# Memory values made token-major after a scan, and local attention with keys and values split once and scaled on VectorE

## The chip, the cores and the metric

The kernel runs on one core of one Trainium2 chip. The metric is device time in microseconds for one execution of the whole program; three runs were timed, and one further execution was profiled. The engines are called as the profile calls them: PE (TensorE matmul), PEld (its weight load), DVE (VectorE), ACT (ScalarE), POOL (GpSimd), SP (SyncE, which issues all the transfers spoken of here).

## What is computed

One encoder layer in float32 on 1024 tokens of width 1024, with 256 memory tokens. The parts that the change touches:

```python
# (A) local attention: 8 heads of 64 in 2 groups of 4, one key and value head per group,
#     blocks of 128 tokens, each block sees itself and its two neighbours, +-128 tokens
scores = einsum('bnqhgd,bnkhd->bnhgqk', qb, kw) * (64 ** -0.5)
m = maximum(max(scores), sink); p = exp(scores - m)
denom = sum(p) + exp(sink - m)
o = einsum('bnhgqk,bnkhd->bnqhd', p / denom, vw)
# (B) gated delta rule, both directions, a scan over chunks
mix = concatenate([attn_o, dn_o]) @ w_out;  x = x + rms_norm(mix)
# cross-attention into the memory tokens
kv = rms_norm(mem) @ w_ckv          # 1024 -> 2048: keys, then values
k, v = kv[..., :1024], kv[..., 1024:]
p = softmax(einsum('bqhd,bkhd->bhqk', q, k) / 16);  c = einsum('bhqk,bkhd->bqhd', p, v) @ w_co
# then a dense SwiGLU
```

## The kernel before, in words

**Precision.** Every large product is made of three products of rounded parts. `split` (L99) writes a rounded copy `hi` on ACT (L102) and the rest `lo = src - hi` on DVE, or on POOL where the caller says so (L103). A product is hi·hi + hi·lo + lo·hi.

**Weights.** `load_w` (L118) loads a block of 512 KB into `wraw` (L125), splits it to `whi` and `wlo`. All three have two buffers, which all matrices share: a third load waits until the first block's split is done, a third split until PE has used the first. `load_w` runs at a raised priority (L120), so its instructions are placed ahead of what stands before them in the program.

**Order.** The program is written as steps in lists (`ORDER_1`, L36, to `ORDER_3`, L38); a scheduler then orders each engine's instructions, and each engine works its list strictly in order and waits at the first instruction whose input or buffer is not ready. In `ORDER_2`, `V` makes the values and `A0` to `A4` the rotated queries and keys of local attention and store them to `d_v`, `d_q`, `d_k`; `W` starts two windows. In `ORDER_3`, `M` normalises and turns the memory tokens into `mT` (two parts, depth on the partitions), `s01` advances both scans by a step, `W` is again two windows, `K` makes one block of the memory's keys or values.

**Local attention** (`window`, L598) works on one block of 128 queries and one group: 16 windows, group 0 first. A window loads its two or three blocks of keys (`kr`, twice, for both halves of the partitions, L610), of queries (`qr`, twice, L611) and of values (`vr`, L613), splits them (`khi` L616, `klo` L617, `vhi` L621, `vlo` L622, `qs` L624 and L625), makes the scores of four heads (`psw`, L633), reduces them on DVE with the mask (L635), takes the exponentials on ACT (L642), the sum (`es`, L645 to L648), and scales the probabilities on ACT (L650). After the `yield` they are turned on PE (`ptw`, L656), split (`ph`, `pl`) and multiplied by the values (`pow`, L661), and the result is stored to `d_mix` (`ao`, L664 to L666). `next_windows` (L668) starts a window before it finishes the one before. The values are kept twice side by side (`vhi` has a dimension of 2), so that `pow` has 128 rows.

**Scan** (`scan`, L749): eight steps for two pairs of heads. Each loads `kv` and `pz`, multiplies 128x128 blocks (`psc`, L763) and updates the state on DVE.

**Keys and values of the memory** (`next_kv`, L883): block `ct` takes 128 columns of `w_ckv` (L125, rows of 512 bytes). The weights are the stationary operand and `mT` with its 256 tokens moves (`pck`, L891): 24 matmuls of 256 columns give a block with 128 features on the partitions. ACT copies it (`cv`, L893). Keys (blocks 0 to 7) go to `d_mk` like that. Values (blocks 8 to 15) are needed with tokens on the partitions, so PE turns them (`ptv`, L899), ACT copies again (`vv`, L901) and SP stores them (L902). `ORDER_3` has eight `K` between the scan steps and eight behind them.

**What follows.** `mid_gemm` (L967) multiplies the mixer's output by `w_out` (`pmg`, L984). Its operand is `d_mix`, loaded (`mraw`, L1023) and split to `b0` to `b3`. Then `mkr` and `mvr` are loaded from `d_mk` and `d_mv` (L1035) and split to `kr` and `vr`, the operands of cross-attention; `gpost` (L961) and `xr` (L994) are loads of a gain and of `x`.

Of the kernel before, what the change touches and what calls it, by code (L numbers as in the profile page):

```python
# [19 lines left out]
P = 128  # L20
S = 1024
D = 1024
KT = D // P
NT = S // P
HALF = 512
# [4 lines left out]
ML = 256  # L30
# [4 lines left out]

ORDER_1 = "D0 P0 D1 P1 D2 P2 D3 P3 B0 B1".split()  # L36
ORDER_2 = "G0 G1 G2 G3 L0 L1 V A4 A0 A1 W L2 L3 W W A2 A3 W".split()
ORDER_3 = ("M " + "s01 W K " * 5 + "s01 K " * 2 + "s01 K s01 " + "K " * 8).split()  # L38


_NAMES = ["ident", "mUi", "mLi", "m5", "m6", "band0", "band1", "band2", "mU", "mL", "ones"]
# [34 lines left out]
def tile_hybrid_block(  # L76
# [31 lines left out]
    def pool(name, bufs, **kw):  # L108
        return tc.tile_pool(name=name, bufs=bufs, reuse_waits="tile", **kw)
# [20 lines left out]


    ident = cst.tile([P, P], F32, name="ident")
# [389 lines left out]
    def levels(h):  # L522
# [72 lines left out]

        together([part(b) for b in range(2)])

    def window(n, g):  # L598

        tok = slice(n * P, (n + 1) * P)  # L600
        k0, k1 = max(n - 1, 0), min(n + 1, NT - 1) + 1
        nb = k1 - k0
        w = nb * P
        band = C[:, _AT["band0"] - C0 + (k0 - n + 1) * P:][:, 0:w]


        kr = tw.tile([P, 384], F32, tag="kr", name="kr", bufs=1)[:, 0:w]
        qr = tw.tile([P, 4, P], F32, tag="qr", name="qr", bufs=1)
        for r in range(2):
            nc.sync.dma_start(kr[64 * r:64 * r + 64], d_k[64 * g:64 * g + 64, k0 * P:k1 * P])  # L610
            nc.sync.dma_start(qr[64 * r:64 * r + 64], d_q[256 * g:256 * g + 256, tok].rearrange("(h e) t -> e h t", h=4))  # L611
        vr = tw.tile([P, 3, 64], F32, tag="vr", name="vr", bufs=1)[:, 0:nb]
        nc.sync.dma_start(vr, d_v[k0:k1, :, 64 * g:64 * g + 64].rearrange("c p e -> p c e"))  # L613
        khi = tw.tile([P, 384], F32R, tag="khi", name="khi")[:, 0:w]
        klo = tw.tile([P, 384], F32R, tag="klo", name="klo", bufs=1)[:, 0:w]
        nc.scalar.copy(khi, kr)  # L616
        nc.gpsimd.tensor_tensor(klo, kr, f32(khi), ALU.subtract)  # L617
        vhi = tw.tile([P, 3, 2, 64], F32R, tag="vhi", name="vhi")[:, 0:nb]
        vlo = tw.tile([P, 3, 2, 64], F32R, tag="vlo", name="vlo")[:, 0:nb]
        v2 = bc(vr, 2, (P, nb, 2, 64))  # L620
        nc.scalar.copy(vhi, v2)  # L621
        nc.gpsimd.tensor_tensor(vlo, v2, f32(vhi), ALU.subtract)  # L622
        qs = tw.tile([P, 4, P], F32R, tag="qs", name="qs")
        nc.scalar.copy(qs, qr)  # L624
        nc.gpsimd.tensor_tensor(qs[64:128], qr[64:128], f32(qs[64:128]), ALU.subtract)  # L625

        m4 = tw.tile([P, 4], F32, tag="m4", name="m4")
        ssum = tw.tile([P, 4], F32, tag="ssum", name="ssum")
        pr = []
        for hh in range(4):  # L630
            pp = pw.tile([P, 512], F32, tag="pw", name="psw")
            for i, kk in enumerate((khi, klo)):
                nc.tensor.matmul(pp[:, 0:w], qs[:, hh, :], kk, start=(i == 0), stop=(i == 1))  # L633
            sc = tw.tile([P, 384], F32, tag="sc", name="sc", bufs=8)
            nc.vector.tensor_tensor_reduce(out=sc[:, 0:w], in0=pp[:, 0:w], in1=band, scale=0.125,  # L635
                                           scalar=sink[:, 4 * g + hh:4 * g + hh + 1], op0=ALU.add, op1=ALU.max,
                                           accum_out=m4[:, hh:hh + 1])
            pr.append(sc)
        nm = tw.tile([P, 4], F32, tag="nm", name="nm")
        nc.vector.tensor_scalar(nm, m4, -1.0, None, ALU.mult)  # L640
        for hh in range(4):
            nc.scalar.activation(pr[hh][:, 0:w], pr[hh][:, 0:w], AF.Exp, bias=nm[:, hh:hh + 1],  # L642
                                 accum_out=ssum[:, hh:hh + 1])
        es = tw.tile([P, 4], F32, tag="es", name="es")
        nc.gpsimd.tensor_tensor(es, sink[:, 4 * g:4 * g + 4], m4, ALU.subtract)  # L645
        nc.scalar.activation(es, es, AF.Exp)
        nc.vector.tensor_tensor(es, es, ssum, ALU.add)
        nc.vector.reciprocal(es, es)  # L648
        for hh in range(4):
            nc.scalar.mul(pr[hh][:, 0:w], pr[hh][:, 0:w], es[:, hh:hh + 1])  # L650
        yield
        po = pw.tile([P, 4, P], F32, tag="pow", name="pow", bufs=1)
        for j in range(nb):
            pp = pw.tile([P, 512], F32, tag="pw", name="ptw")
            for hh in range(4):
                nc.tensor.transpose(pp[:, hh * P:(hh + 1) * P], pr[hh][:, j * P:(j + 1) * P], ident)  # L656
            ph = tw.tile([P, 512], F32R, tag="ph", name="ph")
            pl = tw.tile([P, 512], F32R, tag="pl", name="pl")
            split(ph, pl, pp)
            for i, (vv, pe_) in enumerate(((vhi, ph), (vhi, pl), (vlo, ph))):  # L660
                nc.tensor.matmul(po.rearrange("p h t -> p (h t)"), vv[:, j].rearrange("p r e -> p (r e)"), pe_,  # L661
                                 start=(j == 0 and i == 0), stop=(j == nb - 1 and i == 2))
        ao = tw.tile([P, 2, P], F32, tag="ao", name="ao", bufs=1)
        nc.scalar.copy(ao[0:64], po[0:64, 0:4:2, :])  # L664
        nc.scalar.copy(ao[64:128], po[64:128, 1:4:2, :])
        nc.sync.dma_start(d_mix[g * 256:(g + 1) * 256, tok].rearrange("(k p) t -> p k t", p=P), ao)  # L666

    def next_windows():  # L668

        for _ in range(2):  # L670
            last = wins[-1] if wins else None
            if wins_done[0] < 2 * NT:
                wins.append(window(wins_done[0] % NT, wins_done[0] // NT))
                next(wins[-1])
            wins_done[0] += 1
            if last:
                next(last, None)

    wins, wins_done = [], [0]
    kqv = {0: kqv0}  # L680
# [15 lines left out]
    pw = p12.enter_context(pool("pw", 2, space=PSUM, side="right"))  # L696
    ps = pgs.enter_context(pool("psl", 2, space=PSUM))
    tw = p12.enter_context(pool("tw", 2))
    tl_ = p1.enter_context(pool("tl", 2))

    def attn_proj(ct):
# [179 lines left out]
    kv_done = [0]  # L881

    def next_kv():  # L883

        ct = kv_done[0]
        kv_done[0] += 1
        whi, wlo = load_w(w_ckv[:, ct * P:(ct + 1) * P], KT, P, nc.gpsimd if ct < KT else nc.vector)
# [5 lines left out]
        nc.scalar.copy(cv, pp)  # L893
        if ct < KT:
            nc.sync.dma_start(d_mk[ct * P:(ct + 1) * P, :], cv)
            return
        pt = pc.tile([P, 512], F32, tag="pc", name="ptv")[:, 0:ML]
        for t in range(2):
            nc.tensor.transpose(pt[:, t * P:(t + 1) * P], cv[:, t * P:(t + 1) * P], ident)  # L899
        vv = mk.tile([P, 2, P], F32, tag="vv", name="vv", bufs=2)  # L900
        nc.scalar.copy(vv, pt.rearrange("p (t n) -> p t n", t=2))  # L901
        nc.sync.dma_start(d_mv[:, :, (ct - KT) * P:(ct - KT + 1) * P].rearrange("t p n -> p t n"), vv)  # L902

    scans = [scan(g) for g in range(2)]

    def scan_step(pairs):

        for _ in range(4):
            for s_ in pairs:
                next(s_, None)  # L910

    issue(ORDER_3, {"s": lambda *gs: scan_step([scans[g] for g in gs]), "W": next_windows, "M": memory_norm,
                    "K": next_kv})
    dump("d_pz", d_pz[0] + d_pz[1])
    dump("d_kv", d_kv)
    dump("d_mix", d_mix)
# [454 lines left out]
```

## Time and profile before

| | us |
|---|---|
| median of the 3 runs | 1644.9 (1640.13 to 1646.33) |
| the profiled execution | 1638.65, of which 1636.9 is the span |
| PE busy over the span | 1556.8 (95%) |
| PEld, DVE, ACT, POOL busy | 1305.8, 948.6, 753.1, 547.6 |
| mean granted clock of TensorE | 0.984 |
| first scores of local attention (L633) | 354.1 |
| last value block of the memory (`ptv`, L899) | 619.4 |
| first matmuls of `w_out` (`pmg`, L984) | 619.5 |

The times of the profile are counted from the start of its span. A row of a group of instructions gives line, engine, operation, output and input, then busy time, mean duration of one in ns, idle time of the engine just before them and what ended it. In the timeline a row gives start, duration, engine, line, what it does, and in brackets the idle time before it. The granted clock is a share of full speed. "DMA share" is the mean busy share of the core's 16 transfer engines.

### The profile page before, as it was taken

The numbers are of one execution on the slowest core, as the hardware profiler recorded it, in microseconds if no ns is written. First come the engines' busy times: TensorE is split into PE (matmuls) and PEld (weight loads), VectorE is DVE, ScalarE is ACT, GpSimd is POOL, SyncE is SP. The second block draws the span as 40 slices with busy tenths as digits, with TensorE's granted clock in tenths as the row PEclk, the third lists the DMA queues.
The fourth block names the chain that finished last, engine by engine and source line by source line (L and its number), as shares of the span: only waits on it lengthen the run. The fifth ranks groups of instructions, "written<-read, shape, count | busy, mean of one in ns | idle before, by whom it ended". The sixth has DMA issues, their size and how long they took to land.

```text
span 1636.9 us, 21688 instructions
## 1 busy us (share of the span) xinstructions
PE 1556.8 (95%) x7802; PEld 1305.8 (80%) x7802; DVE 948.6 (58%) x1431; ACT 753.1 (46%) x1530; POOL 547.6 (33%) x501
## 2 busy tenths in 40 slices
PE   6999889998899979999999999999999999999998
PEld 5878778777799877788888777788888888888886
DVE  6855986966678844444346458776555553334332
ACT  6556552236758773554335565233333232444211
POOL 2467552334337500253202221343433441221100
PEclk9999999997999999999999999999999999999999
DMA  6134257574999583454213164442222223565452
GB/s 200 41 116 130 64 167 207 155 176 125 323 315 294 151 288 110 153 182 146 73 65 116 52 217 151 122 135 78 77 91 92 82 84 111 204 213 184 140 173 75
DMA packets 275560, 240.49 MB, mean 147 GB/s; under 512 B 43240, under 2 KB 226941, under 8 KB 275453
## 3 DMA queue, kind: packets, MB, share of 16 engines
q1 hardware_dynamic: 275453, 239.11, 47.0%
q8 instruction: 61, 1.00, 0.2%
q14 instruction: 46, 0.38, 0.1%
HBM read 177.69 MB, written 58.75 MB: 144 GB/s over the span
## 4 chain that ended last, share of the span: by engine, by line
PE 56%; DVE 2%; ACT 1%; issue 1%; DMA 1%; POOL 0%; SPq 0%; POOLq 0%; ACTq 0%; DVEq 0%
PE pmg L984 9%; PE pd L1325 7%; PE pd L1301 7%; PE pD L1155 7%; PE pE L1155 7%; PE pA L1155 6%; PE pcq L260 5%; PE pB L1155 3%; PE pcs L1064 1%; PE pco L1090 1%; DMA wraw<-in_w_gate_up_dram 1%; DVE wlo L103 0%; PE ptn L953 0%; PE pct L1080 0%; ACT xr L1001 0%
## 5 line engine op out<-in xcount | busy, mean ns | idle before, releaser
L102 ACT CAST whi<-wraw 128x1024 fp32r<-128x1024 f32 x108 | 113.1, 1049 | 163.8 <-issue 60.7
L103 POOL TENSOR_TENSOR wlo<-wraw,whi 128x1024 fp32r<-128x1024 f32 x48 | 118.3, 2465 | 173.3 <-ACT whi L102 157.0
L260 PE MATMUL pg<-hhi,whi 128*128 128x512 f32 x352 | 141.0, 402 | 0.0
L260 PE MATMUL pg<-hhi,wlo 128*128 128x512 f32 x352 | 140.3, 399 | 0.0
L260 PE MATMUL pg<-hlo,whi 128*128 128x512 f32 x352 | 140.0, 398 | 0.0
L103 DVE TENSOR_TENSOR wlo<-wraw,whi 128x1024 fp32r<-128x1024 f32 x60 | 74.5, 1244 | 87.5 <-ACT whi L102 83.4
L984 PE MATMUL pmg<-whi,b 128*128 128x512 f32 x384 | 117.7, 396 | 2.9 <-ACT whi L102 2.7
L1155 PE MATMUL pA<-b,whi 128*128 128x512 f32 x352 | 109.5, 392 | 1.3 <-ACT m L1172 1.3
L285 DVE SCALAR_TENSOR_TENSOR acc<-cp,cols,acc 128x1024 f32<-128x1024 f32 x48 | 75.8, 1580 | 34.2 <-ACT acc L283 33.6
L984 PEld LDWEIGHTS pmg<-whi,b 128*128 128x128 f32 x384 | 72.0, 190 | 18.6 <-ACT whi L102 3.5
L1232 POOL TENSOR_TENSOR act<-act,up 128x512 f32<-128x512 f32 x33 | 48.4, 1468 | 108.0 <-issue 58.4
L260 PEld LDWEIGHTS pg<-hhi,wlo 128*128 128x128 f32 x352 | 67.3, 191 | 13.4
L260 PEld LDWEIGHTS pg<-hhi,whi 128*128 128x128 f32 x352 | 67.3, 192 | 13.1 <-ACT hhi L102 0.3
L260 PEld LDWEIGHTS pg<-hlo,whi 128*128 128x128 f32 x352 | 67.1, 191 | 13.1
L1155 PEld LDWEIGHTS pA<-b,whi 128*128 128x128 f32 x352 | 65.3, 188 | 15.0 <-ACT m L1172 2.0
L984 PE MATMUL pmg<-wlo,b 128*128 128x512 f32 x192 | 71.6, 394 | 0.4 <-DVE wlo L103 0.4
L1155 PE MATMUL pA<-b,wlo 128*128 128x512 f32 x176 | 68.7, 391 | 1.0 <-DVE wlo L103 1.0
L1325 PE MATMUL pd<-wdh,ath 128*128 128x512 f32 x176 | 69.5, 395 | 0.0
L1325 PE MATMUL pd<-wdh,atl 128*128 128x512 f32 x176 | 69.4, 395 | 0.0
L1325 PE MATMUL pd<-wdl,ath 128*128 128x512 f32 x176 | 69.4, 395 | 0.0
L1301 PE MATMUL pd<-dl,whi 128*128 128x512 f32 x176 | 68.5, 389 | 0.0
L1301 PE MATMUL pd<-dh,wlo 128*128 128x512 f32 x176 | 68.3, 389 | 0.0
(390 smaller groups left out, 4189.6 us busy)
## 6 DMA issues: line engine op xcount, KB each, us to landing
wraw<-in_w_gate_up_dram SPq DMA_DIRECT2D x52, 512.0 KB, 4.2
kv<-d_kv SPq DMA_DIRECT2D x32, 512.0 KB, 6.5
wraw<-in_w_in_dram SPq DMA_DIRECT2D x22, 512.0 KB, 4.0
araw<-d_act SPq DMA_DIRECT2D x22, 512.0 KB, 3.3
draw<-in_w_down_dram SPq DMA_DIRECT2D x22, 512.0 KB, 4.1
atr<-d_act SPq DMA_DIRECT2D x16, 704.0 KB, 4.7
d_act<-act SPq DMA_DIRECT2D x40, 256.0 KB, 2.8
d_kv<-kv SPq DMA_DIRECT2D x8, 1024.0 KB, 6.4
```

Source lines behind the costliest of these rows:

```text
L102: nc.scalar.copy(hi, src)
L103: (eng or nc.vector).tensor_tensor(lo, src, f32(hi), ALU.subtract)
L260: nc.tensor.matmul(p_, w[:, k, :], ah[a][:, k, :], start=(k == 0 and i == 0), stop=(k == nk - 1 and i == 2))
L285: nc.vector.scalar_tensor_tensor(acc, cp[:, t:t + S], taps[t], acc, ALU.mult, ALU.add)
L984: nc.tensor.matmul(pp[t], act[a][:, k, tt], w_[:, kk, :], start=(k == 0 and i == 0), stop=(k == KT - 1 and i == 2))
L1064: nc.tensor.matmul(pp[:, t2_, :], q[a][:, ct, tt], kr_[b_][:, ct, :], start=(j == 0 and i == 0), stop=(j == 1 and i == 2))
L1090: nc.tensor.matmul(po, vr_[a][:, kt, cs], pts[kt][b_], start=(kt == 0 and i == 0), stop=(kt == 1 and i == 2))
L1155: nc.tensor.matmul(out_, w[a][:, k, :], xx[b_][:, k, :], start=(start and k == 0 and i == 0), stop=(k == HK - 1 and i == 2), skip_group_ch ...
L1232: nc.gpsimd.tensor_tensor(o_, o_, up, ALU.mult)
L1301: nc.tensor.matmul(pps[t], a[:, tt], b_, start=(f == 0 and i == 0), stop=(f == NF - 1 and i == 2))
L1325: nc.tensor.matmul(pp, a[:, f - f0], b_[:, f], start=(f == 0 and i == 0), stop=(f == NF - 1 and i == 2))
```

## The change

Three things, in one diff (cut; line numbers of the new file differ).

1. The values of the memory are made with tokens on the partitions: `mT` is the stationary operand, 512 columns of `w_ckv` move; two steps `V`, of four weight blocks of 256 rows by 512 columns each, stand behind the scan in place of eight `K`. There is no turn; `vv` has one buffer.
2. Keys and values of local attention are loaded and split in halves of 512 tokens for a group (`window_keys`), into tiles that stay; windows read slices. Keys, values and queries share the buffers `wr`, two of them. The values are no longer doubled, and `pow` has 64 rows.
3. The probabilities are scaled by `tensor_scalar` on DVE.

```diff
-ORDER_3 = ("M " + "s01 W K " * 5 + "s01 K " * 2 + "s01 K s01 " + "K " * 8).split()
+ORDER_3 = ("M " + "s01 W K " * 5 + "s01 K " * 3 + "s01 V V").split()
...
+    def window_keys(g, hf):
+        ts, cs = slice(hf * HALF, (hf + 1) * HALF), slice(4 * hf, 4 * hf + 4)
+        kr = tw.tile([P, HALF], F32, tag="wr", name="kr")
+        for r in range(2):
+            nc.sync.dma_start(kr[64 * r:64 * r + 64], d_k[64 * g:64 * g + 64, ts])
+        nc.scalar.copy(khi[:, ts], kr)
+        nc.gpsimd.tensor_tensor(klo[:, ts], kr, f32(khi[:, ts]), ALU.subtract)
+        vr = tw.tile([P, HALF], F32, tag="wr", name="vr")[:, 0:256].rearrange("p (c e) -> p c e", c=4)
+        nc.sync.dma_start(vr, d_v[cs, :, 64 * g:64 * g + 64].rearrange("c p e -> p c e"))
+        nc.scalar.copy(vhi[:, cs], vr)
+        nc.gpsimd.tensor_tensor(vlo[:, cs], vr, f32(vhi[:, cs]), ALU.subtract)
...
     def window(n, g):
...
-        kr = tw.tile([P, 384], F32, tag="kr", name="kr", bufs=1)[:, 0:w]
-        qr = tw.tile([P, 4, P], F32, tag="qr", name="qr", bufs=1)
+        qr = tw.tile([P, 4, P], F32, tag="wr", name="qr")
         for r in range(2):
-            nc.sync.dma_start(kr[64 * r:64 * r + 64], d_k[64 * g:64 * g + 64, k0 * P:k1 * P])
             nc.sync.dma_start(qr[64 * r:64 * r + 64], d_q[256 * g:256 * g + 256, tok].rearrange("(h e) t -> e h t", h=4))
-        vr = tw.tile([P, 3, 64], F32, tag="vr", name="vr", bufs=1)[:, 0:nb]
...
-                nc.tensor.matmul(pp[:, 0:w], qs[:, hh, :], kk, start=(i == 0), stop=(i == 1))
+                nc.tensor.matmul(pp[:, 0:w], qs[:, hh, :], kk[:, ks], start=(i == 0), stop=(i == 1))
...
-            nc.scalar.mul(pr[hh][:, 0:w], pr[hh][:, 0:w], es[:, hh:hh + 1])
+            nc.vector.tensor_scalar(pr[hh][:, 0:w], pr[hh][:, 0:w], es[:, hh:hh + 1], None, ALU.mult)
...
-                nc.tensor.matmul(po.rearrange("p h t -> p (h t)"), vv[:, j].rearrange("p r e -> p (r e)"), pe_,
+                nc.tensor.matmul(po.rearrange("p h t -> p (h t)"), vv[:, k0 + j], pe_,
...
     def next_windows():
         for _ in range(2):
             last = wins[-1] if wins else None
...
+                for hf in range(2) if n == 0 else ():
+                    window_keys(0, hf)
...
+            if n in (NT - 2, NT):
+                window_keys(1, n == NT)
...
+    khi, klo = (tw.tile([P, S], F32R, tag=t, name=t, bufs=1) for t in ("khi", "klo"))
+    vhi, vlo = (tw.tile([P, NT, 64], F32R, tag=t, name=t, bufs=1) for t in ("vhi", "vlo"))
...
-        pt = pc.tile([P, 512], F32, tag="pc", name="ptv")[:, 0:ML]
+    def next_values():
+        ch = kv_done[1]
+        kv_done[1] += 1
+        pp = [pc.tile([P, 512], F32, tag="pc", name="pcv") for _ in range(2)]
+        for kp in range(4):
+            whi, wlo = load_w(w_ckv[kp * 256:(kp + 1) * 256, D + ch * 512:D + (ch + 1) * 512], 2, 512)
+            for t in range(2):
+                for kk in range(2):
+                    k = 2 * kp + kk
+                    for i, (w, a) in enumerate(((whi, 0), (whi, 1), (wlo, 0))):
+                        nc.tensor.matmul(pp[t], mT[a][:, k, t * P:(t + 1) * P], w[:, kk, :], start=(k == 0 and i == 0),
+                                         stop=(k == KT - 1 and i == 2))
         for t in range(2):
-            nc.tensor.transpose(pt[:, t * P:(t + 1) * P], cv[:, t * P:(t + 1) * P], ident)
-        vv = mk.tile([P, 2, P], F32, tag="vv", name="vv", bufs=2)
-        nc.scalar.copy(vv, pt.rearrange("p (t n) -> p t n", t=2))
-        nc.sync.dma_start(d_mv[:, :, (ct - KT) * P:(ct - KT + 1) * P].rearrange("t p n -> p t n"), vv)
+            vv = mk.tile([P, 512], F32, tag="vv", name="vv", bufs=1)
+            nc.scalar.copy(vv, pp[t])
+            nc.sync.dma_start(d_mv[t, :, ch * 512:(ch + 1) * 512], vv)
```

More of the change, by code (lines that the diff above doesn't have):

```diff
@@ L604, in window @@
         band = C[:, _AT["band0"] - C0 + (k0 - n + 1) * P:][:, 0:w]
-        kr = tw.tile([P, 384], F32, tag="kr", name="kr", bufs=1)[:, 0:w]
-        qr = tw.tile([P, 4, P], F32, tag="qr", name="qr", bufs=1)
+        ks = slice(k0 * P, k1 * P)
+        qr = tw.tile([P, 4, P], F32, tag="wr", name="qr")
         for r in range(2):
-            nc.sync.dma_start(kr[64 * r:64 * r + 64], d_k[64 * g:64 * g + 64, k0 * P:k1 * P])
             nc.sync.dma_start(qr[64 * r:64 * r + 64], d_q[256 * g:256 * g + 256, tok].rearrange("(h e) t -> e h t", h=4))
-        vr = tw.tile([P, 3, 64], F32, tag="vr", name="vr", bufs=1)[:, 0:nb]
[L613 to L622, printed above, removed]
         qs = tw.tile([P, 4, P], F32R, tag="qs", name="qs")
@@ L649, in window @@
         for hh in range(4):
-            nc.scalar.mul(pr[hh][:, 0:w], pr[hh][:, 0:w], es[:, hh:hh + 1])
+            nc.vector.tensor_scalar(pr[hh][:, 0:w], pr[hh][:, 0:w], es[:, hh:hh + 1], None, ALU.mult)
         yield
-        po = pw.tile([P, 4, P], F32, tag="pow", name="pow", bufs=1)
+        po = pw.tile([P, 4, P], F32, tag="pow", name="pow", bufs=1)[0:64]
         for j in range(nb):
@@ L660, in window @@
             for i, (vv, pe_) in enumerate(((vhi, ph), (vhi, pl), (vlo, ph))):
-                nc.tensor.matmul(po.rearrange("p h t -> p (h t)"), vv[:, j].rearrange("p r e -> p (r e)"), pe_,
+                nc.tensor.matmul(po.rearrange("p h t -> p (h t)"), vv[:, k0 + j], pe_,
                                  start=(j == 0 and i == 0), stop=(j == nb - 1 and i == 2))
         ao = tw.tile([P, 2, P], F32, tag="ao", name="ao", bufs=1)
-        nc.scalar.copy(ao[0:64], po[0:64, 0:4:2, :])
-        nc.scalar.copy(ao[64:128], po[64:128, 1:4:2, :])
+        for r in range(2):
+            nc.scalar.copy(ao[64 * r:64 * r + 64], po[:, r:4:2, :])
         nc.sync.dma_start(d_mix[g * 256:(g + 1) * 256, tok].rearrange("(k p) t -> p k t", p=P), ao)
@@ L671, in next_windows @@
             last = wins[-1] if wins else None
-            if wins_done[0] < 2 * NT:
-                wins.append(window(wins_done[0] % NT, wins_done[0] // NT))
+            n = wins_done[0]
+            if n < 2 * NT:
+                for hf in range(2) if n == 0 else ():
+                    window_keys(0, hf)
+                wins.append(window(n % NT, n // NT))
                 next(wins[-1])
@@ L879, in memory_norm, with next_keys @@
                 split(mT[0][:, k, :], mT[1][:, k, :], pt[:, i], gain("mem", k))
-    kv_done = [0]
-    def next_kv():
+    kv_done = [0, 0]
+    def next_keys():
         ct = kv_done[0]
         kv_done[0] += 1
-        whi, wlo = load_w(w_ckv[:, ct * P:(ct + 1) * P], KT, P, nc.gpsimd if ct < KT else nc.vector)
+        whi, wlo = load_w(w_ckv[:, ct * P:(ct + 1) * P], KT, P, nc.gpsimd)
         pp = pc.tile([P, 512], F32, tag="pc", name="pck")[:, 0:ML]
@@ L893, in next_kv @@
         nc.scalar.copy(cv, pp)
-        if ct < KT:
-            nc.sync.dma_start(d_mk[ct * P:(ct + 1) * P, :], cv)
-            return
-        pt = pc.tile([P, 512], F32, tag="pc", name="ptv")[:, 0:ML]
+        nc.sync.dma_start(d_mk[ct * P:(ct + 1) * P, :], cv)
+    def next_values():
[10 more added lines that the diff above has]
+                                         stop=(k == KT - 1 and i == 2))
         for t in range(2):
-            nc.tensor.transpose(pt[:, t * P:(t + 1) * P], cv[:, t * P:(t + 1) * P], ident)
-        vv = mk.tile([P, 2, P], F32, tag="vv", name="vv", bufs=2)
-        nc.scalar.copy(vv, pt.rearrange("p (t n) -> p t n", t=2))
-        nc.sync.dma_start(d_mv[:, :, (ct - KT) * P:(ct - KT + 1) * P].rearrange("t p n -> p t n"), vv)
+            vv = mk.tile([P, 512], F32, tag="vv", name="vv", bufs=1)
+            nc.scalar.copy(vv, pp[t])
+            nc.sync.dma_start(d_mv[t, :, ch * 512:(ch + 1) * 512], vv)
     scans = [scan(g) for g in range(2)]
@@ L912, in tile_hybrid_block @@
     issue(ORDER_3, {"s": lambda *gs: scan_step([scans[g] for g in gs]), "W": next_windows, "M": memory_norm,
-                    "K": next_kv})
+                    "K": next_keys, "V": next_values})
     dump("d_pz", d_pz[0] + d_pz[1])
```

## The prediction, made before the changed kernel had run

> **What bounds the kernel now.** I read the page first, then a table of stages, the waits of PE, the chain, and the timeline around each wait. The page's chain is 56% PE, but from the mixer's output projection (`pmg`) on PE's instructions stand in the same order in both kernels, so the change is decided between 354 us (first scores of local attention) and 634 us. The table of stages shows start:end, length, then busy time of PE, PEld, DVE, ACT and POOL, granted clock, DMA share and GB/s:
>
> ```profile
> 354.00:434.00 80.00, 68.77 (x364) 58.95 (x364) 51.24 (x127) 55.46 (x145) 30.89 (x35) 0.83 0.60 186
> 434.00:550.00 116.00, 113.89 (x901) 109.14 (x900) 89.52 (x247) 84.57 (x237) 65.41 (x67) 1.00 0.94 286
> 550.00:622.00 72.00, 58.52 (x392) 53.61 (x392) 41.17 (x73) 53.63 (x122) 10.55 (x15) 0.93 0.70 218
> 622.00:716.00 94.00, 90.89 (x408) 74.46 (x407) 44.53 (x46) 40.68 (x68) 14.68 (x22) 0.98 0.40 131
> ```
>
> Three stages, three limits. 354 to 434: PE idles 11.2 us and runs at 0.83. 434 to 550 (the scan): PE is busy 98% at clock 1.00, although transfers are busy 0.94. 550 to 622 (end of the scan, values of the memory tokens): PE idles 13.5 us. The waits of PE from 600 to 634 (total, times, longest) name the cause:
>
> ```profile
> PE ptv L899 <- ACT cv L893: 7.8, 3, 4.1
> PE pmg L984 <- ACT whi L102: 0.5, 1, 0.5
> ```
>
> PE turns each value block right after it is made, so it waits for ACT's copy, and ACT stands behind splits whose data has not landed. The chain shows how the stage ends:
>
> ```profile
> 620.24 1.98 DMA d_mv<-vv
> 622.23 5.96 DMA mvr<-d_mv
> 628.22 1.92 ACT vr L102
> ...
> 633.64 6.42 PE pmg L984 x27
> ```
>
> The values go out to DRAM, come back and are split. Now this costs PE about 1 us only (0.9 idle from 622 to 634): two blocks of `w_out` and all mixer operands are split before that wait, and PE multiplies from 619.5 on.
>
> **Values, 8 blocks to 2.** PE loses 192 matmuls of 256 columns at 0.120 us from start to start (566.6 to 570 us) and 16 turns at 0.147, 23.0 + 2.4 = 25.4 us; it gains 96 of 512 columns at 0.227 (528 `pd` matmuls in 119.7 us) = 21.8. ACT: 16 copies of 0.37 become 4 of 0.58. The loads stay 8 of 512 KB, but each block is now a quarter of the depth, so half the columns are finished only with the fourth block.
>
> **Keys and values split once.** 32 + 16 loads become 8 + 4; 4.2 MB becomes 1.5; at 286 GB/s 9 us of transfers, and 36 issues of 0.42 us leave SP. ACT loses about 15.6 us of casts and adds 4.0, POOL loses 30 us of subtractions and adds 9. All of it runs in stages whose end PE sets, so I count it at nothing between 434 and 550; if transfers paced that stage it would be worth up to 9 us (a rival). One shared ring of two buffers (`wr`) now serves keys, values and queries; the keys come first in it and need only `A4` and `V`, earlier than `A0` and `A1`, which the queries need, so I count no wait; if a query's load waited for the last key piece it would be a cast and a subtraction, 0.6 + 1.3 us, once.
>
> **Scaling moved.** ACT loses 32.4 us:
>
> ```profile
> L650 ACT ACTIVATE sc<-sc,es 128x384 f32<-128x384 f32 x48 | 25.7, 613 | 1.1 <-DVE es L648 1.1
> ```
>
> (plus 16 narrower; they overlap, four take 2.13 or 1.70). DVE has no such row. Its nearest are L385 (128x512 with a column as factor, 0.483) and L869 (128x1024, 0.748): 0.52 ns a column, so 0.417 for 384 and 0.35 for 256, 25.6 us in all. There is a price beside it:
>
> ```profile
> 471.40 2.35 POOL L103 TENSOR_TENSOR wlo<-wraw,whi 128x1024 fp32r<-128x1024 f32 x1 [2.06 <-ACT whi L102]
> 471.49 2.28 DVE L647 TENSOR_TENSOR es<-es,ssum 128x4 f32<-128x4 f32 x1
> ```
>
> An instruction of 0.16 us took 2.28 and ended with POOL's. Over 16 the mean is 0.306 against a median of 0.164: 0.14 extra each. Bounds for one scaling: 0.35 and 0.42 + 2.35. I take 0.42 + 0.14, so 35 us in all, 2.2 a window.
> [...]
>
> **354 to 434.** PE's waits there are DVE 3.0, ACT 3.0, transfers 2.7, the rest small. ACT gets rid of about 3 us a window, DVE takes 2.2. The wait for `pz` stays: the order still puts the first scan matmuls behind it. Between +2 (DVE's wait grows) and -11 (all idle time goes), I take **-3**, the part of ACT.
>
> **434 to 550.** DVE has 26.5 us idle; about 7.25 windows x 2.2 us = 16 fill it to 91%. PE waits there 2 us in all now. Between 0 (cover holds) and +20 (each scaling meets half of a 2.35 us subtraction: 7.25 x 4 x 1.6 = 46 us against 26.5 idle), nearer the former: **+4**.
>
> **The end.** In the changed order one window more stands behind the last scan step: 8 score matmuls at 0.17, 12 turns at 0.147, 9 at 0.233 = 5.3 us, so the last step's turns (566.3 us now; call it E) come **-5.3**. Then, from the new E:
> - `gpost` is issued at 3.5 as now (569.85). Ahead of the sixth value block in SP's order stand five mixer loads, four of `x`, `mkr` and the fifth block. Now the same crowd, issued from 569.85, lets a block land at 594.3: 24.4 us for 7 MB. At the 351 GB/s of 572 to 595 it is 20. So it lands at 26; before that PE has windows and the first five blocks, nearly without idling.
> - ACT's cast ends at 27.5, DVE's at 28.9, PE's matmuls of it at 30.7, of the seventh block 33.7. The eighth load is issued at 29.2 (its buffer is freed by the sixth's split), lands in 4.1, is split at 35.5, done at 37.3.
> - The last window's exponentials stand behind that split on DVE, so ACT copies the first half of the values at 39.4, not at 37.9. `vv` has one buffer: the second copy waits for the first store (1.98 at best) and ends at 42.9; behind it on ACT stand the last turned probabilities, for which PE waits, and the split of the keys. Store 2.0, reload 5.96, split 1.92: 53.2.
> - New: in the built order this split stands **ahead of every mixer split** (`b`) on ACT, and its low half ahead of them on DVE. So `pmg` starts with four matmuls at 53.2 + 1.05 = 54.2 and goes on at 53.2 + 2.28 + 1.23 = 56.7; less the 0.9 us already done, 55.8. Queued behind it are the third and fourth `w_out` casts; they come in time (10.9 us of matmuls are ready by then).
> - PE has idled about 10 us by then. After 4.1 us idle it ran at half speed from 614.5 to 617.7 now (0.215 instead of 0.120 a matmul), 1.5 us lost; I add 1.7: 57.5.
>
> Now it is 619.5 + 0.9 - 566.3 = 54.1 us. So **+3.4**: the 8 us of `ptv` waits go and about 10 us in front of `pmg` take their place.
>
> **Sum.** -3 + 4 - 5.3 + 3.4 = -0.9. The profiled execution took 1638.65 us (span 1636.9); by it the changed kernel takes 1637.8. The runs' median, 1644.9, is 6 us above that execution, so I give 1644. Within 0.5% (8.2 us) nothing can be told from no change.
>
> **Rivals.**
> - *The reload ahead of the mixer splits sets the end* (slower). The stores and the reload land late: medians of 4.7 us, at most 9.4, are seen for `d_mv<-vv`. Two stores at 4.7 to 7 give +5.4 to +10; the eighth block at 6.1 instead of 4.1 gives +2. With -0.9: +7 to +11, 1654. It decides as soon as E to `pmg` exceeds 54.1 + 5.3 + 8 = 67 us. For it: nothing else can feed PE then. Against: transfers have thinned by then (0.58 from 595 to 622).
> - *VectorE becomes the bound of the scan* (slower): the +20 above, mechanism in the `es` row, from the point where scalings average over 1 us (26.5 us of cover by 29 scalings); 1656 to 1660. Against: POOL loses 21 us, and one `es` in sixteen was held so long. [...]
> - *ACT was the pace at the start, or transfers that of the scan* (faster): the 11 us idle of 354 to 434 go with half the clock loss there (0.17 x 69 = 12 us), or 9 us of transfers: -9 to -16, 1632. For: ACT is 82% busy from 400 to 434. Against: PE is 98% busy in the scan.
> - *The change does not shorten the value stage* since it waits for the same transfers: that is my forecast.
>
> **Chances.** Forecast 0.52 (1637 to 1652); reload 0.17; VectorE 0.12; faster 0.19. So faster 0.19, same 0.52, slower 0.29. For 8 in 10 the range reaches to 1632 and 1657.
>
> **What would show it.** `ptv` gone; one wait of ACT for `mvr` with PE idle 8 to 12 us in front of the first `pmg`; scalings near 0.42 to 0.56; DVE above 88% and PE above 95% from 434 to the last step. Wrong if PE's wait before `pmg` is under 4 us, if scalings average over 1 us, or if the scan stage changes by over 8 us.

## The result, and the profile after

| | before | changed |
|---|---|---|
| median of 20 runs each, us | 1640.34 (1635.16 to 1646.64) | 1646.84 (1642.29 to 1650.47) |
| ratio, 95% interval | 1 | 1.0036 (1.0026 to 1.0046) |
| profiled execution, us | 1638.65 | 1643.5 |
| E, the first of the last scan step's four turns | 566.3 | 560.1 |
| first matmul of `w_out` (`pmg`) | 619.5 | 622.2 |

The changed kernel is slower by 0.36%, 5.9 us by this ratio (the medians differ by 6.5); forecast were -0.9. Executions of the kernel before lie up to 6 us on either side of their median, so below the ratios say how much. The traces, one execution each, say where, and differences of a few us between two traces can be such scatter.

First the table of stages of the changed kernel, with cuts that answer to those of before (start:end, length, busy time of PE, PEld, DVE, ACT, POOL, granted clock, DMA share, GB/s):

```profile
360.00:428.00 68.00, 56.41 (x318) 46.89 (x318) 51.28 (x127) 38.21 (x101) 23.55 (x24) 0.87 0.61 188
428.00:544.00 116.00, 112.88 (x889) 106.08 (x888) 96.62 (x276) 63.47 (x192) 52.17 (x57) 1.00 0.88 273
544.00:622.00 78.00, 58.50 (x305) 44.64 (x303) 51.73 (x104) 46.93 (x105) 5.84 (x10) 0.91 0.67 221
622.00:720.00 98.00, 95.57 (x417) 78.70 (x418) 44.65 (x47) 41.08 (x69) 14.75 (x22) 0.95 0.34 110
```

The scan stage is nearly what it was: PE busy 112.9 of 116 us (113.9 before), ACT 21 us less, DVE 7 us more. The third stage, the end of the scan and the values, is where PE idles: 19.5 us, where it was 13.5. The waits of PE from 600 to 634 (total, times, longest):

```profile
PE pmg L1003 <- ACT b L102: 10.8, 1, 10.8
PE pow L661 <- ACT ph L102: 1.5, 1, 1.5
PE pow L661 <- DVE pl L103: 1.0, 1, 1.0
```

The 7.8 us of `ptv` are gone, and one wait of 10.8 us in front of the first `pmg` stands in their place. The timeline around it (start, duration, engine, line, what; in brackets the idle time before and what ended it):

```profile
609.28 0.41 SPq L1054 DMA_DIRECT2D mvr<-d_mv  x1
609.38 1.90 ACT L102 CAST kr<-mkr 128x2048 fp32r<-128x2048 f32 x1
610.96 0.40 PE L661 MATMUL pow<-ph,vlo 128*64 128x512 f32 x1
611.43 0.74 ACT L665 COPY ao<-pow 64x256 f32<-64x256 f32 x2 [0.15 <-PE pow L661]
612.20 0.36 SPq L666 DMA_DIRECT2D d_mix<-ao  x1
612.65 2.85 SPq L1042 DMA_DIRECT2D mraw<-d_mix  x3
614.56 1.90 ACT L102 CAST vr<-mvr 128x2048 fp32r<-128x2048 f32 x1 [2.38 <-DMA mvr<-d_mv]
616.36 7.67 ACT L102 CAST b<-mraw 128x1024 fp32r<-128x1024 f32 x8
622.19 2.50 PE L1003 MATMUL pmg<-whi,b 128*128 128x512 f32 x5 [10.84 <-ACT b L102]
```

Three things are to be seen. The reload's cast (`vr`) stands ahead of the mixer's eight casts (`b`), as forecast. But `pmg` starts with the end of the **sixth** of them (622.14; one starts every 0.947 us and takes 1.04), not of the first. And three of the eight mixer loads are issued only at 612.65, right after the last window's last matmul (610.96) and its store.

The program says why. The mixer's operand is loaded in quarters; those of local attention for the first 512 tokens (`kp` 0 and 1, with which `pmg` begins) go to a buffer of their own, `raw01`, which lies where the windows' tiles lie:

```python
raw = raw01 if hf == 0 and kp < 2 else raws[hf]
nc.sync.dma_start(raw[:, k2, :], d_mix[kp * 256:(kp + 1) * 256, hf * HALF:(hf + 1) * HALF]...)
split(mxT[hf][0][:, k2, :], mxT[hf][1][:, k2, :], raw[:, k2, :])
```

The first of these two loads (612.65) waits for the semaphore that PE's last `pow` matmul raises (611.35), and their casts come sixth and seventh on ACT. So load, cast and `pmg` hang on the last window. What stands on PE between that window and `pmg`, the cover, decides whether this is seen; in the traces that is:

```
before:  ... pow6 pck22 ptv2 pck24 ptv2 pck24 ptv2 | pmg     (some 70 matmuls and 6 turns)
changed: ... pow3 ptw4 pow4 ptw4 pow2 ptw4 pow6     | pmg     (nothing)
```

### The profile page after: what moved, and what is told of

It is laid out like the page before. It is cut to its first block, busy times and chain, and to the rows that moved or that the text cites. A ratio compares the mean times of both kernels' runs of the same rounds, so it can differ in the third digit from the quotient of the medians.

```text
span 1641.8 us, 21290 instructions
## 1 busy us (share of the span) xinstructions
PE 1554.6 (95%) x7690; PEld 1291.5 (79%) x7690; DVE 967.7 (59%) x1495; ACT 711.0 (43%) x1430; POOL 526.9 (32%) x477
```

## The experiments

**Theory A (the seam).** The loss lies between E and `pmg`, in the seam where one stage hands over to the next: the changed order puts the last window last on PE and the reload ahead of the mixer's casts. **Rival B**: the token-major values themselves are the loss, by their one buffer and late reload. **Rival C**: the scalings slow the scan stage through DVE. All ratios are to the kernel before in the same set of runs; the last three columns are us in the one trace of each, with E counted here at the start of the last of the four turns (566.6 before, 560.5 in the changed kernel). The work between E and `pmg` is not the same in all of them, since windows move past E; the last two columns are the surer ones.

| kernel | ratio, 95% | E to first `pmg` | last window's last matmul to first `pmg` | PE's wait right in front of the first `pmg` |
|---|---|---|---|---|
| before | 1 | 52.9 | 21.7 | none |
| changed | 1.0036 (1.0026 to 1.0046) | 61.7 | 11.2 | 10.8 |
| `p1_values_only` | 0.9978 (0.9967 to 0.9990) | 49.6 | 11.8 | 11.4 |
| `p2_split_once` | 0.9997 (0.9981 to 1.0014) | 50.9 | 15.6 | none |
| `p3_scale_vector` | 1.0023 (1.0010 to 1.0035) | 56.7 | 10.5 | 1.6 |
| `p23_windows_only` | 1.0062 (1.0045 to 1.0079) | 62.7 | 11.2 | 10.8 |
| `scale_on_scalar` (1 and 2) | 1.0016 (1.0004 to 1.0029) | 48.9 | 11.2 | 10.8 |
| `reload_late` | 1.0057 (1.0041 to 1.0073) | 60.2 | 8.2 | 7.8 |
| `own_buffer` | 1.0004 (0.9991 to 1.0017) | 58.6 | 7.7 | 7.1 |
| `own_buffer_pool` | 1.0015 (1.0000 to 1.0029) | 56.6 | 7.7 | 7.3 |
| `p1_own_buffer` | 0.9964 (0.9945 to 0.9984) | 49.1 | 12.0 | 8.9 |
| `before_own_buffer` | 1.0013 (0.9998 to 1.0028) | 56.2 | 20.8 | none |
| `cover_values` | 1.0006 (0.9992 to 1.0021) | 60.1 | 16.4 | 3.4 |
| `seam_free` | 0.9982 (0.9970 to 0.9994) | 54.7 | 2.3 | 1.9 |
| `p1_best` | 0.9946 (0.9926 to 0.9965) | 43.6 | 6.8 | 3.7 |
| `scale_seam_free` | 0.9927 (0.9908 to 0.9946) | 40.7 | 2.3 | 1.9 |

### Parts alone and undone

`p1_values_only` is the kernel before with `next_values` and the new `ORDER_3`; `p23_windows_only` the changed kernel with `next_kv` and the old one; `scale_on_scalar` the changed kernel with

```diff
-            nc.vector.tensor_scalar(pr[hh][:, 0:w], pr[hh][:, 0:w], es[:, hh:hh + 1], None, ALU.mult)
+            nc.scalar.mul(pr[hh][:, 0:w], pr[hh][:, 0:w], es[:, hh:hh + 1])
```

> The kernel before with the token-major values alone; keys and values of the windows are split per window and scaled on ScalarE as before. The two kernels stand at 1640.3 (before) and 1646.8 us (changed). Theory A (the seam): the changed kernel loses between the last scan step's turns and the first matmul of the mixer (pmg), because in its built order the last window comes last on PE, and the values' reload is split ahead of all mixer operands. In this kernel the built order on ScalarE has the last window ahead of the last value copies and the mixer's casts ahead of the reload's: the 8 us of ptv waits and 3.6 us of matmuls go and nothing takes their place, so 1631 to 1636 us, and PE idles under 3 us in front of pmg. Rival B (the values are the loss: one buffer, store and reload end late): 1645 to 1649 us, and 8 us or more idle in front of pmg here too. Rival C (scalings on VectorE slow the scan stage): as A in time, but the gain lies from 430 to 550 us.

> The changed kernel with the values of the memory made as before (8 blocks with turns), so keys and values split once and scaling on VectorE alone. In its built order the last window stands behind the last value block's work and the reload's cast of the keys ahead of the mixer's casts, as in the changed kernel. Theory A: the end of the stage is as late as in the changed kernel although no value block changed, 1642 to 1648 us. Rival B: without the token-major values the loss is gone, 1634 to 1639 us. Rival C: 1644 to 1650 us, with the loss from 430 to 550 us.

> The changed kernel with the 64 scalings back on ScalarE, nothing else. Built order on ScalarE: the last window's end ahead of the last value copy, five mixer casts ahead of the first reload cast. Theory A: the scalings on VectorE cost nothing where they stand, but they move the last window behind the values; undoing them brings the window and the mixer's casts forward, so 1632 to 1638 us, and the first scores to last scan step take as long as in the changed kernel within 2 us. Rival B: 1645 to 1649 us, since values and reload stay. Rival C: 1636 to 1641 us with the gain in the scan stage, and pmg still waiting 8 us or more.

Rival B falls: the values alone make the kernel faster by 0.22%, and without them parts 2 and 3 lose 0.62%. Theory A has the sign of these two right, but not its detail: I had expected no wait of `pmg` in the first, and it is there in all of them. Waits of PE from 600 to 640, first `p1_values_only`, then `p23_windows_only`:

```profile
PE pmg L994 <- ACT b L102: 11.4, 1, 11.4
```

```profile
PE pmg L993 <- ACT b L102: 10.8, 1, 10.8
PE ptv L908 <- ACT cv L902: 2.2, 2, 1.8
```

In the second the values are made as before, and still `pmg` waits: here, too, no value block is left on PE behind the last window. Its time alone (1648.2 us) would fit Rival C as well (1644 to 1650). In its trace PE's idle time grew by 5.9 us between E and `pmg` (17.3 against 11.4) and by 2.1 between the first scan matmul and E (8.0 against 5.9), so the larger part lies in the seam and a smaller one may be C's. `scale_on_scalar` missed A's range (1632 to 1638 us; measured 1640.8, against 1637.8 before): its last window comes 7 us earlier than in the changed kernel, and `pmg` waits 10.8 us after it all the same. The wait goes with the last window, wherever that is.

### The reload taken away

```diff
         for hl, raw, src in ((kr_, ..., d_mk...), (vr_, ..., d_mv...)):
-        nc.sync.dma_start(raw, src)
+        with tc.issue_after(stores[0].ins):     # on SP behind the first store of x1
+            nc.sync.dma_start(raw, src)
         split(*hl, raw)
```

> The changed kernel with the reload of the memory's keys and values (mkr, mvr) issued on SP behind the first store of x1, far behind the first pmg, so that no cast of it stands ahead of the mixer's. Theory A, as refined by the trace: the first pmg also waits for the mixer rows whose buffer (raw01) is freed only by the last window's last matmul (their loads were issued at 612.65 us); with the reload gone this still holds, so 2 to 4 us of the 10.8 us wait go: 1642.5 to 1645 us. Rival B1 (the reload alone is the loss): 6 to 10 us go, 1637 to 1641 us. Rival (neither): 1646.8.

No gain (1.0057, where 1642.5 to 1645 us, a ratio of 1.001 to 1.003, was expected and the changed kernel has 1.0036 in its own set of runs), so the reload ahead of the casts is not by itself the loss. In its timeline ACT has nothing of the reload any more, and yet:

```profile
616.45 1.91 SPq L1043 DMA_DIRECT2D mraw<-d_mix  x3
621.88 1.04 ACT L102 CAST b<-mraw 128x1024 fp32r<-128x1024 f32 x1 [1.07 <-DMA mraw<-d_mix]
622.98 2.50 PE L1004 MATMUL pmg<-whi,b 128*128 128x512 f32 x5 [7.85 <-ACT b L102]
```

The sixth cast now waits for its load, which is issued behind the last window. From there to `pmg` it takes 8.2 us instead of 11.2: the refined theory's 3 us. They are lost again behind: the two casts of the reload now stand among those of `w_out`, PE waits 4.8 us for `whi` there (2.2 in the changed kernel), and from the first `pmg` to the first matmul of cross-attention's queries (`pcq`) it takes 101.2 us (97.6 in the changed kernel).

### The place of the mixer's rows

**Theory A2.** `pmg` starts 8 to 12 us after the last window because load and cast hang on the place of `raw01`. The unused half of the tile's own buffer takes that away without touching a wait:

```diff
-            raw = raw01 if hf == 0 and kp < 2 else raws[hf]
+            raw = raws[hf]
```

`own_buffer_pool` also splits `kr` and `vr` on POOL (a copy and a subtraction there); `p1_own_buffer` has the same line in `p1_values_only`; `before_own_buffer` is the control.

> The changed kernel, but the mixer's rows of local attention for the first half of the tokens are loaded into the unused half of their own tile instead of raw01, whose place is freed only by the last window's last matmul. Theory A2 (formed from the traces so far): in all five kernels pmg starts 8.3 to 11.8 us after the last window's last matmul, whatever stands before, because load, cast and pmg hang on that place; so the loads now come some 40 us earlier, and pmg waits for the reload's cast alone, which still stands ahead: 616.5 + 1.05 instead of 622.2, 4 to 5 us less than the changed kernel (ratio to before 1.000 to 1.002, where it has 1.0036). Rival B (the reload's cast ends the wait, raw01 hides behind it): no gain, 1.003 to 1.005. Rival D (the mixer operands wait for data of the last window, not for the place): no gain either, and the loads stay at 612 us.

> As own_buffer, and the reload of the memory's keys and values is split on GpSimd, which is idle there, so that neither cast stands ahead of the mixer's on ScalarE or VectorE. Theory A2: nothing is left in front of pmg but the last window's own matmuls, so PE idles under 3 us there; pmg starts near 612 us, 9 to 11 us less than the changed kernel: ratio 0.996 to 0.998. If the place and the reload are not the cause, 1.002 or more.

> The kernel before with the token-major values alone (p1_values_only, 0.9978) and the mixer's rows in their own tile. There pmg waited 11.4 us after the last window (605.8 to 617.6). Theory A2: the wait goes, the mixer's casts stand ahead of the reload's already, pmg starts at 606 to 609 us: another 8 to 11 us, ratio 0.991 to 0.993. If the wait is for something else: 0.997 to 0.998.

> The kernel before with the mixer's rows in their own tile, nothing else: the control. There the value blocks (pck, ptv) stand behind the last window on PE and cover the load and the casts, so theory A2 expects no change: 0.999 to 1.001, pmg within 1 us of 619.5. If the own tile speeds the kernel by itself (some other effect of the buffer), it would show here as 0.997 or less.

The line takes 0.32% (5.3 us, by ratios from two sets of runs) off the changed kernel, the 4 to 5 us expected, and nothing off the kernel before, where the value blocks cover it; that control came out a little above its range (1.0013, interval 0.9998 to 1.0028, where 0.999 to 1.001 was expected), and its first `pmg` came at 628.7, not within 1 us of 619.5. So A2 holds by the ratios; in the traces 3.1 us of the gain lie between E and `pmg`. Rival D falls as well, since the loads of these rows are now issued from 569.8 on. What is left in `own_buffer` is the reload's cast, and here the last window's copy behind it:

```profile
622.20 1.90 ACT L102 CAST vr<-mvr 128x2048 fp32r<-128x2048 f32 x1 [6.34 <-DMA mvr<-d_mv]
624.00 0.74 ACT L665 COPY ao<-pow 64x256 f32<-64x256 f32 x2
624.77 7.68 ACT L102 CAST b<-mraw 128x1024 fp32r<-128x1024 f32 x8
```

`own_buffer_pool` missed its range by far (0.996 to 0.998; measured 1.0015). With `vr` off ACT the wait did not go, it changed its owner:

```profile
619.33 0.74 ACT L665 COPY ao<-pow 64x256 f32<-64x256 f32 x2 [6.88 <-DMA d_mix<-ao]
620.09 7.67 ACT L102 CAST b<-mraw 128x1024 fp32r<-128x1024 f32 x8
620.85 4.56 POOL L1056 TENSOR_TENSOR kr<-mkr,kr 128x2048 fp32r<-128x2048 f32 x1
621.24 17.57 DVE L103 TENSOR_TENSOR b<-mraw,b 128x1024 fp32r<-128x1024 f32 x8 [8.07 <-ACT b L102]
```

`ao` has one buffer, so the last window's copy waits for the store of the window before it, and that store was issued right behind the reload of 1 MB. And DVE's eight subtractions take 17.6 us instead of 9.2 while POOL subtracts (below); PE then waits another 3.3 us for the first of them. `p1_own_buffer` missed, too (0.991 to 0.993 expected): a third owner, the PSUM bank that the last value copy frees, behind seven casts on ACT:

```profile
PE pmg L994 <- ACT vv L911: 8.9, 1, 8.9
```

### One part alone, and the seam taken apart

`p2_split_once` and `p3_scale_vector` are the kernel before with one part. `seam_free` is the changed kernel with the own buffer, the reload behind the first store of `x1` and split on POOL, and the second value copy in two pieces through the idle key buffers:

```diff
-            vv = mk.tile([P, 512], F32, tag="vv", name="vv", bufs=1)
+            parts = ((512, "vv", 1),) if t == 0 else ((ML, "cv", 2), (ML, "cv", 2))
```

`p1_best` is `p1_values_only` with the own buffer, the split on POOL and these pieces.

> The kernel before with the windows' keys and values split once, nothing else (values of the memory and scalings as before). Theory A3 (what counts is the work that stands on PE behind the last window's last matmul, since the mixer's load and cast hang on that matmul): here two value blocks with their turns (48 and 4 matmuls) still stand behind it, so the load and the cast are covered: ratio 0.998 to 1.002. Rival E (part 2 costs by itself: first scores 5 us later, as all traces with it show, or the shared ring of raw tiles): 1.003 to 1.006, with the loss already at the last scan step's turns.

> The kernel before with the 64 scalings on VectorE, nothing else. In its built order 22 of the last window's matmuls moved behind, and one value block of 24 matmuls with 2 turns is left behind the last window, some 3 to 7 us of cover for the 8 to 11 us that load and cast take. Theory A3: 1.001 to 1.004, with a wait of pmg of 2 to 7 us, and the scan stage unchanged within 2 us. Rival C (VectorE slows the scan): the same ratio, but the last scan step's turns come later and pmg waits no longer than before. Rival (no cost at all): 0.998 to 1.000.

> The changed kernel with the whole seam taken apart: mixer rows in their own tile, the reload of keys and values issued behind the first store of x1 and split on GpSimd, and the second half of each value chunk copied through the two idle key buffers so that no copy waits for a store. own_buffer (1.0004) still waited 7.1 us in front of pmg, there for the reload's cast, in own_buffer_pool (1.0015) for ScalarE's copy of the last window, which waited 6.9 us for the store of the window before it, queued behind the reload. Theory A3: nothing of that is left, PE idles under 3 us in front of pmg, 4 to 6 us less than own_buffer: 0.996 to 0.998. If still 7 us of wait are there or the ratio is 1.000 or more, something else holds the seam.

> The kernel before with the token-major values alone, the mixer rows in their own tile, the reload split on GpSimd and the last value copies through the idle key buffers. In p1_own_buffer (0.9964) the first pmg waited 8.9 us for a bank that the last value copy frees, behind seven casts. Here the value copies stand ahead of the casts, 12 matmuls of values stand behind the last window, and neither cast of the reload is on ScalarE. Theory A3: PE idles under 3 us in front of pmg, 0.991 to 0.994. If the wait comes back in another place: 0.996 to 0.998.

Alone the parts give -0.22, -0.03 and +0.23% (each give or take 0.1 to 0.2), in sum nothing; together +0.36%. Most of the difference is the seam, as `cover_values` below shows: in `p2_split_once` two value blocks and in `p3_scale_vector` one are left behind the last window, and the first `pmg` waits not at all and 1.6 us (the `ptv` waits of the kernel before stay, 7.6 and 6.2 us from 600 to 640).

Where part 3's own price lies is not settled. The 1.6 us are less than the 2 to 7 expected. From the first scores to E it takes 210.6 us (212.5 before) and from E to `pmg` 3.8 us more, but 27 matmuls of windows moved past E, 4.9 us at the pace of the prediction, so the stage up to E took some 3 us longer for its work, not shorter (a rough reading, since the first scores do not stand at the same place in PE's work). From 434 to 560 us PE idles 4.8 us, before 2.1, so Rival C is not excluded as a part of it (first the kernel before, then `p3_scale_vector`):

```profile
434.00:560.00 126.00, 123.87 (x981) 118.67 (x979) 98.12 (x266) 91.69 (x259) 70.58 (x73) 1.00 0.89 272
434.00:560.00 126.00, 121.21 (x957) 116.26 (x958) 103.98 (x292) 72.57 (x211) 68.43 (x70) 1.00 0.90 272
```

`p1_best` missed its range narrowly (0.9946; 0.991 to 0.994 expected): `pmg` still waits 3.7 us there for the first mixer cast. `seam_free` (0.9982, at the edge of its 0.996 to 0.998) makes the changed kernel as a whole faster than before; the one long wait is gone:

```profile
PE pmg L1006 <- ACT b L102: 1.9, 1, 1.9
```

### Still open then: cover, and parts 1 and 2 together

`cover_values` is the changed kernel with 48 value matmuls queued on PE behind the last window, no buffer and no load changed; `scale_seam_free` is `scale_on_scalar` with the seam taken apart as in `seam_free`; `scale_again` is a second trace of `scale_on_scalar`.

```diff
+                        with tc.issue_after(pow_last[0].ins) if ch == 1 else nullcontext():
                             nc.tensor.matmul(pp[t], mT[a][:, k, t * P:(t + 1) * P], w[:, kk, :], ...)
```

> The changed kernel with one edge more: the 48 matmuls of the second value chunk are queued on PE behind the last window's last matmul; no buffer and no load is changed. 48 x 0.227 = 10.9 us of PE work then cover the 8 to 11 us that the mixer's load and cast take after that matmul, and in the built order the mixer's casts stand ahead of the reload's. Theory A3: PE's wait of 10.8 us in front of pmg goes, some of it comes back while PE waits for the windows without values to fill in (2 to 5 us): ratio 0.998 to 1.001, where the changed kernel has 1.0036. Rival (cover is not the point, PE is just late by the sum of its work): 1.003 to 1.005.

> scale_on_scalar (parts 1 and 2, 1.0016) with the seam taken apart as in seam_free. If what part 2 costs beside part 1 lies in the seam, this comes down to p1_best: 0.993 to 0.996. If part 2 costs before the last scan step (first scores 5 us later), it stays 0.3% above p1_best: 0.997 to 0.999.

> The same kernel as scale_on_scalar, for a second trace. Its first trace was of the fastest run (1634.9 us; the median of 12 was 1640.8). If runs differ in the seam, this trace shows the last scan step's turns within 2 us of the first trace's (565.9), relative to the first scores, and pmg later than 614.9 us by about the difference of the two times. If they differ before, the first scores or the last scan step are late by as much.

Moving work behind the last window is enough to bring the changed kernel back to 1.0006; PE's wait in front of the first `pmg` falls from 10.8 to 3.4 us, now for a bank:

```profile
PE pmg L1005 <- ACT vv L922: 3.4, 1, 3.4
```

`scale_seam_free` beats both kernels: 1631.4 us against 1644.0 of the kernel before in the same set of runs, 0.73% by the ratio, a little better than expected. `p1_best`, without part 2, has 0.9946, and the intervals overlap: no price of part 2 beside part 1 is seen once the seam is apart, though the two also differ in the reload, which `p1_best` leaves in its place. Why parts 1 and 2 together measured 1.0016 is not settled: `scale_again` (1638.1 us) is 3.3 us slower than the first trace and spreads it: 0.7 up to the first scores, 1.7 from there to E, -0.5 from E to `pmg`, 1.4 behind. Neither expectation holds. With the seam apart, part 3 still separates 0.9982 from 0.9927, so its price is not only the seam; 3.6 us are longer waits of `pow` for `ph` and `pl` (7.4 against 3.8 us from 540 us on in the two traces), the rest is not located.

## Why the prediction was wrong, point by point

- **Values, 8 blocks to 2**: right on the work. 25.4 against 21.8 us on PE; alone it gives -3.6 us. That the two agree so well is partly luck: the 8 us of `ptv` waits went, and a wait of 11.4 us took their place even there.
- **Keys and values split once at nothing**: right on the time, 0.9997 alone (0.9981 to 1.0014, so up to 3 us either way are not excluded). In the stage it was not nothing: in that trace PE idles 5.6 us from 434 to 560, where it was 2.1.
- **Scalings at 0.42 + 0.14 us**: the 0.42 was right, the price for POOL too high. The 48 wide ones took 0.455 us in the mean with a median near 0.41, so 0.04 extra, since POOL held only four of the 64 (last section). That a scaling would be held like `es`, by 0.14 in the mean, was my estimate from the `es` row, and no run shows it. The rival of VectorE as the bound falls in its strong form, which needed over 1 us: DVE is busy 86% from 434 us to the last step (over 88% was expected), PE 96%.

```profile
L650 DVE TENSOR_SCALAR sc<-sc,es 128x384 f32<-128x384 f32 x48 | 18.8, 455 | 0.1
L650 DVE TENSOR_SCALAR sc<-sc,es 128x256 f32<-128x256 f32 x16 | 4.5, 347 | 0.1
```

- **E**: -3 + 4 - 5.3 = -4.3 forecast, -6.2 measured. The sum is right within the scatter, but not by its terms, and that is luck. The -3 did not come: PE idles 11.6 of 68 us there, before 11.2 of 80. Of the +4 some came: 5.4 us idle from 434 to 560, before 2.1. What moved E is mainly the window work behind it, 34 matmuls worth 6.3 us at the forecast's pace, where 5.3 were counted, and a better clock at the start (0.87 of full there, 0.83 before).
- **The end, +3.4: the step that failed.** First `pmg` was put at E + 54.2, it came at E + 62.1. Of the 7.9 us, 3.2 are the chain that I did follow: the `vr` split ended at E + 56.4, not 53.2, since the last value copy ended at E + 45.8 (42.9) and `mvr` was issued at E + 49.2 (45.3), behind the store of `ao` on SP; the reload itself was 0.7 us quicker than counted. The other 4.7 are five more casts: I took it that `pmg` starts with the first `b` cast, and it needs the sixth. The order on ACT was read, but not which of the eight casts the first matmul uses, nor that its load had not been issued.
- The cause named, the reload ahead of the mixer's casts, was half of it. `reload_late` shows that without it the load behind the last window holds `pmg` almost as long. In the part of the prediction on what bounds the kernel, "all mixer operands are split before that wait" was noted for the kernel before; that the last window moves behind the last value block, and takes them along, was not. I counted that window as 5.3 us moved past E; it also uncovered 8 to 11 us of load and cast (the last window's last matmul to the first `pmg`).
- **The rival "reload sets the end"** had the sign and nearly the size (+7 to +11 against +5.9), but not the place, and its point of 67 us from E was not reached (62.1).
- **The clock**: 1.7 us were added for half speed after the wait. It was more. From 622 to 628 and from 628 to 640:

```profile
622.00:628.00 6.00, 5.81 (x14) 4.56 (x15) 5.74 (x5) 2.03 (x3) 0.00 (x0) 0.51 0.00 0
628.00:640.00 12.00, 12.00 (x55) 9.90 (x54) 3.70 (x4) 2.11 (x2) 0.00 (x0) 1.00 0.19 53
```

14 matmuls in 5.8 us at a granted clock of 0.51, where 14 at the pace of the second row (12.0 / 55) take 3.1: 2.7 us for one wait of 10.8.

## What to carry to other kernels

For a stage that begins behind a seam, look up which load and which cast its **first** matmul needs and what frees the buffer they go to, then count the work that stands on the engine between that event and the matmul. An edit that shortens or reorders work which waits for nothing can cost more than it saves if that work was the cover; here three edits worth -0.22, -0.03 and +0.23% alone gave +0.36% together, and 48 matmuls put back behind the event undid it. When a wait is taken away, name the next one in the queue before counting the gain: in front of the same matmul four owners stood one behind the other (the place of a buffer, the reload's cast, the one-buffer store, a PSUM bank).

## What the runs showed of the hardware that was not expected

DVE and POOL held each other up in `own_buffer_pool`, where both subtracted, with two SBUF inputs each. Two of DVE's eight subtractions, 1.22 us each in `seam_free`, took 5.25 and 5.59 us and ended 1.08 us after POOL's two (620.85 to 625.41, 625.36 to 630.92): by these times each was held until POOL's instruction was over. POOL's second took 5.56 us, where the same took 4.63 in `seam_free`. DVE's eight together took 17.6 us instead of the 9.2 of `seam_free`.

The scalings, one SBUF input and a factor for each row, were held in the same way, but seldom. In the changed kernel four of the 64 began while POOL worked on two inputs of 256 columns or more; they took 0.58 to 1.20 us and ended 0.21 to 0.22 us after POOL's instruction, one of them here. All others took 0.34 to 0.42.

```profile
509.91 1.18 POOL L847 TENSOR_TENSOR ol<-ol,ors 128x512 f32<-128x512 f32 x1
510.10 1.20 DVE L650 TENSOR_SCALAR sc<-sc,es 128x384 f32<-128x384 f32 x1
```

In the kernel before, where ACT scales, 15 scalings began so, over 0.3 us ahead of the end of POOL's instruction, and none was held (0.50 to 0.62 us, as the others). Why DVE's four were held and none of ACT's is not shown.

After the wait of 10.8 us PE ran at a granted clock of 0.50 for 5.7 us, from 622.19 to 627.9, and then at 1.00 (the two rows above, cut at 628, give 0.51 and 1.00); by the timeline single `pmg` matmuls took 0.63 us there and 0.39 behind. In four other traces with such a wait the first shorter matmul began 4.8 to 6.1 us after the first `pmg`: 4.8 in `p1_values_only` (wait of 11.4 us), 4.9 in `p1_own_buffer` (8.9), 5.7 in `scale_on_scalar` (10.8), 6.1 in `reload_late` (7.8). In `own_buffer_pool`, where PE waited once more in between, for 3.3 us, a matmul still took 0.63 us at 628.84, 7.65 us after the start of the first. What sets the length is not shown; it does not grow with the wait in these traces.
